# One core, fp32 decoder in split precision: two blocks' wide products behind each other, then both blocks' narrow ones, and later stages

## The chip, the cores and the metric

The kernel runs on one core of a Trainium2 chip. The metric is the device time of one execution in microseconds (us). One core has a matrix engine (TensorE, PE in the profile, with PEld for its weight loads), a vector engine (VectorE, DVE), a scalar engine (ScalarE, ACT), GpSimd (POOL) and SyncE (SP), which issues most transfers here. Each engine takes its own queue in order; they wait for each other by semaphores.

## The reference

Two decoder layers on 256 tokens of width 2048, all in fp32. Layer 0 has forgetting attention ("FoX": 32 heads of 64, a bias from a running sum of log-sigmoids), layer 1 attention in a window of 128 (32 query heads, 4 key/value heads, a learned sink per head, partial rotary). Both have a SiLU gate and an output projection.

```python
for i in range(DEPTH):
    h = rmsnorm(x, norm_g[i])
    if i % N_MIXERS == 0:
        p = h @ fox_w_in[j]            # q, k, v, gate, forget: 2048 x 8224
        ...
        y = fox_attention(q, k, v, log_f)
        w_out = fox_w_out[j]
    else:
        p = h @ swa_w_in[j]            # q, k, v, gate: 2048 x 4608
        ...
        y = swa_attention(q, k, v, swa_sinks[j])
        w_out = swa_w_out[j]
    y = y * jax.nn.silu(gate)
    x = x + y @ w_out
return rmsnorm(x, final_g)
```

## The kernel before

**Products.** Every fp32 operand is split into a high and a low half (two fp32r numbers), and a product keeps three of the four partial products. A `Unit` is 256 columns of an output; its 16 k-tiles come in parts of at most four. A part's weights are loaded by SP (`load`, L188 to L208), ACT casts the high half (L204), DVE subtracts to get the low half (L205). `block(unit, p, c)` (L210 to L248) does one part for one half `c` of the unit's 256 rows or columns: for each k-tile a **wide** matmul, 128x512, of the high stationary half with both halves of the moving operand side by side, and then for each k-tile a **narrow** one, 128x256, of the low stationary half with the high moving half. A block of four k-tiles is thus four wide and four narrow matmuls into one PSUM tile `acc`. After a unit's last part, `consume` is called: ACT copies the low columns out (L252), DVE adds, and what follows depends on the unit (q, k, v, gate, output). Units whose moving operand is the weight (v) read `acc<-w,xs` in the profile; the others read `acc<-xs,w`; in the output projections `ys` stands in place of `xs`. Matmuls are issued in one line (L75), transposes in L78.

**The order.** PE's order is the program's. The main loop (L876 to L889) takes the stream of (unit, part) and for each one emits half 0 of that part, and then half 1 of the part before it; only the last unit of the stream is done otherwise. So four wide, four narrow of one block are followed by four wide, four narrow of another. Inside a block `tick` (L104) is called after every second matmul: a block of four k-tiles is four **steps**. `after(n, f)` puts `f` n steps later; this is how the attention's stages are laid between the products. The other engines' order is set by the scheduler when the program is built; what a stage emits has a higher priority there (`HP`, L26).

**The stages of FoX.** When the first half of a group's k is consumed, `attend` (L404) puts off the two pairs of heads of the group (8 groups of 4 heads) by a table: `FOX_FIRST` for group 0, `FOX_NEXT` for group 1, `FOX_DUE` for the rest, `SWA_DUE` in layer 1. An entry (s, t) stands for: scores `s` after s steps, transposes `t` after t steps (the second head's four steps later); the third entry is when the values' products (`psy`) are done. `s` (L338) does two 128x512 matmuls into two PSUM tiles `ps_s`, DVE adds the bias (L347) and reduces (L333). The second block of keys (`s_first`, L353) follows `SECOND` = 8 steps later: two 128x256 matmuls into one `ps_s`, DVE add and reduce (L358, L333), then the softmax: L533 and L534 on DVE, four exponentials on ACT (L290), the reciprocal (L298) and four normalising products (L301) on DVE. The `ps_s` pool has two buffers. `t` (L363) transposes three blocks of the normalised `st` into `pt` (L78), ACT copies them (L369). The v unit's `consume` scales by ACT into `vg` (L462) and adds by DVE (L463), once for each half.

**Between the layers**, after each output row ACT and DVE split the new `x` for layer 1 (L155, L156), ACT squares it (L599), GpSimd sums the squares (L605); `norm` is put off by 10 steps after the last row (L629) and begins with the `ps_n` matmuls over that sum.

Of the kernel before, what the change touches and what calls it, by code (L numbers as in the profile page):

```python
# [36 lines left out]
SCALE_DUE = 8  # L37


FOX_DUE = ((16, 44), (48, 74), 106)  # L40
FOX_FIRST = ((60, 88), (86, 114), 128)
FOX_NEXT = ((28, 56), (58, 88), 112)
SWA_DUE = ((16, 40), (44, 64), 74)

SECOND = 8
WBUFS = 5
# [7 lines left out]
def trunk(  # L54
# [19 lines left out]
    def mm(*args, **kw):  # L74
        tc.keep_in_program_order(nc.tensor.matmul(*args, **kw))  # L75
# [24 lines left out]
    due = {}  # L100

    def after(steps, fn):
        due.setdefault(clock[0] + max(steps, 1), []).append(fn)

    def tick():
        clock[0] += 1
        for fn in due.pop(clock[0], ()):
            with tc.high_priority(HP):
                fn()
# [19 lines left out]
    def inv_rms(sums, name, columns, ps):  # L129
        for i, a in enumerate(sums):  # L130
            mm(ps[:, 0:S], ones, a, start=i == 0, stop=i == len(sums) - 1)
        n = S
        if columns:
            n = S + 2
            for th in range(2):
                for i, a in enumerate(sums):
                    mm(
                        ps[:, S + th : S + th + 1], a[:, th * P : (th + 1) * P], ones[:, 0:1],
                        start=i == 0, stop=i == len(sums) - 1,
                    )  # L140
        v = cpool.tile([P, S + 2], F32, tag="rms_v", name=f"v_{name}")[:, 0:n]
        nc.vector.tensor_scalar(v, ps[:, 0:n], 1.0 / D, EPS, op0=ALU.mult, op1=ALU.add)
        r = cpool.tile([P, S + 2], F32, tag="rms_r", name=f"r_{name}", bufs=2)[:, 0:n]
        nc.scalar.activation(r, v, AF.Ln)
        nc.scalar.activation(r, r, AF.Exp, scale=-0.5)

        t = cpool.tile([P, S + 2], F32, tag="rms_t", name=f"t_{name}")[:, 0:n]
        nc.vector.scalar_tensor_tensor(out=t, in0=r, scalar=-0.5, in1=r, op0=ALU.mult, op1=ALU.mult)
        nc.vector.tensor_mul(t, t, v)
        nc.vector.scalar_tensor_tensor(out=r, in0=t, scalar=1.5, in1=r, op0=ALU.add, op1=ALU.mult)  # L150
        return r

    def split_x(kt, layer):
        g = g_sb[:, layer, kt : kt + 1]
        nc.scalar.activation(xs[:, kt, 0, :], xT[:, kt, :], AF.Copy, scale=g)  # L155
        nc.vector.scalar_tensor_tensor(  # L156
            out=xs[:, kt, 1, :], in0=xT[:, kt, :], scalar=g, in1=xs[:, kt, 0, :].bitcast(F32),
            op0=ALU.mult, op1=ALU.subtract,
        )
# [50 lines left out]
    def block(unit, p, c):  # L210
        _, _, _, kt0, s = unit.parts[p]
        w, a = loaded[unit, p], unit.acts
        if p == 0:
            pool, tag = unit.acc
            unit.ps[c] = pool.tile([P, 512], F32, tag=tag, name="acc")
        n = unit.n if unit.kind == "tok" else S
        both, ps = unit.ps[c], unit.ps[c][:, 0:n]
        cs = slice(c * P, (c + 1) * P)
        def operands(i):

            kt = kt0 + i
            if unit.kind == "tok":
                return a[:, kt, 0, cs], a[:, kt, 1, cs], w[:, i]
            return w[:, i, 0, cs], w[:, i, 1, cs], a[:, kt]

        first, last = kt0 == 0, kt0 + s == KT
        ops = [operands(i) for i in range(s)]
        if unit.halves:

            for i, (sh, _, mv) in enumerate(ops):  # L230
                mm(both, sh, mv.rearrange("p h n -> p (h n)"), start=first and i == 0, stop=False)
                if i % 2:
                    tick()
            if s % 2:
                tick()
            for i, (_, sl, mv) in enumerate(ops):
                mm(ps, sl, mv[:, 0, :], start=False, stop=last and i == s - 1)
                if i % 2:
                    tick()
        else:  # L240
            for i, (sh, sl, mv) in enumerate(ops):
                mm(ps, sh, mv[:, 0, :], start=first and i == 0, stop=False)
                mm(ps, sl, mv[:, 0, :], start=False, stop=False)
            for i, (sh, _, mv) in enumerate(ops):
                mm(ps, sh, mv[:, 1, :], start=False, stop=last and i == s - 1)
                tick()
        if p == len(unit.parts) - 1:
            unit.consume(c, unit.ps[c])  # L248

    def low_half(ps):  # L250
        s = work.tile([P, S], F32, tag="row", name="half", bufs=4)
# [62 lines left out]
    class Pair:  # L314
# [23 lines left out]
        def s(self):  # L338

            self.st = work.tile([P, 2, 3 * P], F32, tag="st", name="st")  # L340
            self.mx = work.tile([P, 2, 2], F32, tag="mx", name="mx")
            rng, qb = BLK[1]
            pss = [ps_s.tile([P, 512], F32, tag="S", name="ps_s") for _ in range(2)]
            for hh in range(2):
                self.product(pss[hh], hh, qb, S)
            for hh in range(2):
                nc.vector.tensor_add(self.st[:, hh, rng], pss[hh][:, S:], self.bias[:, hh, rng])  # L347
                self.reduce(pss[hh][:, 0:S], hh, rng, qb)
            after(SECOND, self.s_first)

        def s_first(self):

# [15 lines left out]
                group.pts[hh] = work.tile([P, 2, 3 * P], F32, tag=f"pts{hh}", name="pts", bufs=1)  # L368
            nc.scalar.copy(group.pts[hh][:, self.j, :], pt[:, 0 : 3 * P])  # L369

        def later(self, group, s, t):
            after(s - BIAS, self.early)
            after(s, self.s)
            after(t, lambda: self.t(0, group))
            after(t + 4, lambda: self.t(1, group))
# [25 lines left out]
    class Group:  # L401


        def attend(self, kt, due, shared):  # L404
            self.pts = [None, None]
            for j, (s, t) in enumerate(due[0:2]):
                self.pair(j).later(self, s, t)
            after(due[2], lambda: self.values(kt, shared))

        def values(self, kt, shared):  # L410
# [56 lines left out]
    class FoxGroup(Group):  # L467
# [13 lines left out]
        def k(self, c, ps):  # L481
# [11 lines left out]
            if c == 0:  # L493
                due = {0: FOX_FIRST, 1: FOX_NEXT}.get(self.g, FOX_DUE)
                self.attend(2 * self.g, due, False)
# [101 lines left out]
    def square_into(sums, m):  # L597
        s = work.tile([P, S], F32, tag="row", name="sq", bufs=4)
        nc.scalar.activation(s, xT[:, m, :], AF.Square)  # L599
        if m == 0:  # L600
            acc = cpool.tile([P, S], F32, tag="ssq", name="acc", bufs=2)
            sums.append(acc)
            nc.gpsimd.tensor_copy(acc, s)  # L603
        else:
            nc.gpsimd.tensor_add(sums[0], sums[0], s)  # L605
# [5 lines left out]
    def to_layer1(m):  # L611
        split_x(m, 1)
        square_into(sums1, m)
        if m == KT - 1:

            def norm():
                nonlocal swa
                fox_scope.__exit__(None, None, None)
                swa = ctx.enter_context(tc.tile_pool(name="swa", bufs=2))
                state["r1"] = r = inv_rms(  # L620
                    sums1, "n1", True, ps_s.tile([P, 512], F32, tag="S", name="ps_n1")
                )
                rope = swa.tile([P, 2, S], F32, name="rope_c", bufs=1)
                nc.sync.dma_start(out=rope, in_=rope_d)
                nc.vector.tensor_mul(rope, rope, r[:, 0:S].unsqueeze(1).to_broadcast([P, 2, S]))
                state["rr"] = rope
                after(20, tail_residual)

            after(10, norm)  # L629

# [78 lines left out]

    fox_units = units
    first_out = out_units(fox_out_d, to_layer1)


# [32 lines left out]
    class SwaGroup(Group):  # L748
# [6 lines left out]
        def q(self, c, ps):  # L755
# [3 lines left out]
            if c == 0:  # L759
                self.attend(2 * self.u, SWA_DUE, True)  # L760

# [32 lines left out]
    last_out = out_units(swa_out_d, to_end)  # L794
# [46 lines left out]
    start = [(u, p) for p in range(2) for u in (v0, q0, k0)] + [(v0, 2), (v0, 3), (q0, 2), (k0, 2)]  # L841
# [7 lines left out]
    def fetch(upto):  # L849
        while fetched[0] < min(upto, len(stream)):  # L850
            load(*stream[fetched[0]])
            fetched[0] += 1
# [20 lines left out]
    sink = cpool.tile([P, H], F32, name="sink")  # L873
    state["sink"] = sink

    prev = None  # L876
    for i, (u, p) in enumerate(stream):
        fetch(i + 1 + LOOK)
        if u is last_out[7]:
            if p == 0:  # L880
                block(*prev, 1)
            block(u, p, 0)
            continue
        block(u, p, 0)
        if prev is not None:
            block(*prev, 1)
        prev = (u, p)
    for p in range(len(last_out[7].parts)):
        block(last_out[7], p, 1)  # L889


# ---- launch: one core; the host only lays arrays out
# [62 lines left out]
```

## Time and profile before

| | |
|---|---|
| median of 3 runs | 840.53 us (839.79 to 840.77) |
| profiled execution | 840.97 us, of which the traced span is 838.8 us |
| mean granted TensorE clock | 0.997 |
| PE busy, matmuls | 826.1 us, 98% of the span, 4906 |
| DVE busy | 670.3 us, 80% |
| ACT busy | 543.6 us, 65% |
| waits of PE, all | 6.9 us |

A timeline row reads: start (us from the span's start), us, engine, line, operation, output<-inputs, shape of the first instruction and the number of instructions put together in the row; in brackets the engine's idle time before it and who ended it. A matmul's listed end is modelled and lies past the start of the next one; spacing is read from starts. Steps are not marked in the profile; a block of four k-tiles is eight matmuls.

### The profile page before, as it was taken

The page shows a single profiled execution, that of the slowest core. Times are in us where ns is not written, and L with a number is a line of the kernel's source. Part 1 is how long each engine was busy: PE and PEld are TensorE (multiplying, and loading weights), DVE is VectorE, ACT ScalarE, POOL GpSimd, SP SyncE. Part 2 cuts the span into 40 slices and gives each one's busy share as a digit, 9 for nine tenths or more (in the row PEclk, how much of TensorE's full clock was granted, in tenths as well). Part 3 has the DMA queues.
Part 4 walks back from the last instruction along what each step waited for, and adds up shares of the span by engine and source line. Part 5 has one row for each costly group of instructions (what it writes and reads, how often), then busy time and mean ns, then how long its engine had stood idle before and what let it go on. Part 6 is the DMA issues. An engine that isn't in the chain of part 4 may idle for free.

```text
span 838.8 us, 13409 instructions
## 1 busy us (share of the span) xinstructions
PE 826.1 (98%) x4906; PEld 715.7 (85%) x4906; DVE 670.3 (80%) x1424; ACT 543.6 (65%) x1062; POOL 61.1 (7%) x93
## 2 busy tenths in 40 slices
PE   8999999999999999999999999999999999999996
PEld 7888888888888888888888888888888888888885
DVE  5899888779696887968658778788898889876755
ACT  6687776667575675757546565567766776665652
POOL 1011100100000010000002110000000000001311
PEclk9999999999999999999999999999999999999998
DMA  8666554655555465544475554544444445346522
GB/s 275 229 227 237 191 181 171 216 185 204 157 206 183 164 221 164 218 159 145 157 240 180 195 201 156 188 160 138 164 151 151 158 144 163 124 146 232 195 101 100
DMA packets 26672, 150.49 MB, mean 179 GB/s; under 512 B 3264, under 2 KB 5472, under 8 KB 11248
## 3 DMA queue, kind: packets, MB, share of 16 engines
q1 hardware_dynamic: 24192, 142.22, 49.5%
q0 software_dynamic: 1408, 6.36, 2.3%
q10 hardware_dynamic: 1008, 1.07, 0.4%
q8 instruction: 38, 0.62, 0.3%
q14 instruction: 26, 0.21, 0.1%
HBM read 147.50 MB, written 2.15 MB: 178 GB/s over the span
## 4 chain that ended last, share of the span: by engine, by line
PE 91%; DVE 3%; DMA 2%; ACT 2%; issue 1%; SPq 1%; DVEq 0%; ACTq 0%
PE acc L75 82%; PE ps_s L75 3%; PE psy L75 3%; PE pt L78 3%; DMA wraw<-in_fox_in_dram 1%; DVE w L205 1%; DMA wraw<-in_vf_dram 1%; ACT w L204 1%; SPq L199 1%; DVE xs L156 0%; ACT sq L818 0%; DVE scaled L699 0%; DVE ssq L819 0%; SPq L807 0%; DVE kk L490 0%
## 5 line engine op out<-in xcount | busy, mean ns | idle before, releaser
L75 PE MATMUL acc<-xs,w 128*128 128x256 f32 (+1 forms) x2624 | 485.2, 339 | 0.4 <-ACT w L204 0.3
L75 PEld LDWEIGHTS acc<-xs,w 128*128 128x128 f32 x2624 | 407.2, 189 | 61.3 <-issue 3.9
L205 DVE TENSOR_TENSOR w<-wraw,w 128x1024 fp32r<-128x1024 f32 (+4 forms) x275 | 324.1, 1183 | 96.3 <-ACT w L204 93.9
L204 ACT CAST w<-wraw 128x1024 fp32r<-128x1024 f32 (+4 forms) x275 | 277.8, 1015 | 153.2 <-PE acc L75 127.7
L75 PE MATMUL acc<-ys,w 128*128 128x512 f32 x960 | 170.4, 338 | 0.0
L75 PEld LDWEIGHTS acc<-ys,w 128*128 128x128 f32 x960 | 147.4, 189 | 21.5 <-issue 0.6
L75 PE MATMUL acc<-w,xs 128*128 128x256 f32 (+2 forms) x608 | 114.9, 334 | 1.9 <-ACT w L204 1.7
L75 PEld LDWEIGHTS acc<-w,xs 128*128 128x128 f32 x608 | 94.6, 189 | 14.8 <-ACT w L204 2.7
L252 ACT COPY half<-acc 128x256 f32<-128x256 f32 x112 | 41.2, 368 | 45.0 <-PE acc L75 44.3
L290 ACT ACTIVATE st<-st,mx 128x128 f32<-128x128 f32 (+1 forms) x128 | 56.6, 444 | 10.7 <-DVE mx L534 5.4
L369 ACT COPY pts<-pt 128x384 f32<-128x384 f32 x64 | 30.4, 475 | 14.5 <-PE pt L78 14.5
L75 PE MATMUL ps_s<-kk,q 128*128 128x512 f32 (+2 forms) x192 | 35.2, 306 | 1.3 <-DVE mx L333 1.3
L605 POOL TENSOR_TENSOR acc<-acc,sq 128x256 f32<-128x256 f32 x28 | 29.5, 1053 | 88.8 <-ACT sq L599 88.8
L301 DVE TENSOR_SCALAR st<-st,rl 128x128 f32<-128x128 f32 (+1 forms) x128 | 32.9, 321 | 1.1
L78 PE MATMUL pt<-ident,st 128*128 128x128 f32 x192 | 31.4, 272 | 0.0
L75 PEld LDWEIGHTS ps_s<-kk,q 128*128 128x128 f32 x192 | 26.2, 190 | 2.2 <-issue 1.7
L603 POOL COPY acc<-sq 128x256 f32<-128x256 f32 x2 | 1.9, 936 | 342.8 <-ACT sq L599 342.8
L521 POOL DMA_DIRECT2D bc<-negc_d x16 | 8.8, 553 | 221.0 <-DVE st L358 170.6
L78 PEld LDWEIGHTS pt<-ident,st 128*128 128x128 f32 x192 | 23.1, 140 | 1.9
L156 DVE SCALAR_TENSOR_TENSOR xs<-xT,g_sb,xs 128x256 fp32r<-128x256 f32 x32 | 22.0, 710 | 3.2 <-ACT xs L155 3.0
L310 ACT CAST q<-qT 64x256 fp32r<-64x256 f32 x32 | 12.8, 400 | 17.8 <-DVE qT L729 17.4
L290 ACT ACTIVATION_READ_ACCUMULATOR st<-st,mx 128x1 f32 x128 | 23.9, 187 | 0.0
(136 smaller groups left out, 590.7 us busy)
## 6 DMA issues: line engine op xcount, KB each, us to landing
wraw<-in_fox_in_dram SPq DMA_DIRECT2D x58, 1024.0 KB, 4.9
wraw<-in_swa_in_dram SPq DMA_DIRECT2D x36, 1024.0 KB, 4.9
wraw<-in_fox_out_dram SPq DMA_DIRECT2D x13, 1024.0 KB, 4.9
wraw<-in_swa_out_dram SPq DMA_DIRECT2D x13, 1024.0 KB, 4.9
bc<-negc_d POOLq DMA_DIRECT2D x16, 384.0 KB, 4.0
wraw<-in_fox_out_dram SPq DMA_DIRECT2D x6, 512.0 KB, 3.7
wraw<-in_swa_out_dram SPq DMA_DIRECT2D x6, 512.0 KB, 3.7
wraw<-in_fox_in_dram SPq DMA_DIRECT2D x4, 512.0 KB, 6.0
```

What stands on the lines that cost most here:

```text
L75: tc.keep_in_program_order(nc.tensor.matmul(*args, **kw))
L78: tc.keep_in_program_order(nc.tensor.transpose(out, in_, ident))
L156: nc.vector.scalar_tensor_tensor(out=xs[:, kt, 1, :], in0=xT[:, kt, :], scalar=g, in1=xs[:, kt, 0, :].bitcast(F32), op0=ALU.mult, op1=ALU. ...
L204: state["split"] = nc.scalar.copy(w[:, :, 0, :], raw)
L205: nc.vector.tensor_tensor(out=w[:, :, 1, :], in0=raw, in1=w[:, :, 0, :].bitcast(F32), op=ALU.subtract)
L252: nc.scalar.copy(s, ps[:, S : 2 * S])
L290: nc.scalar.activation(st[:, hh, rng], st[:, hh, rng], AF.Exp, bias=nm[:, qb, hh : hh + 1], accum_out=l[:, qb, hh : hh + 1],)
L301: nc.vector.tensor_scalar_mul(st[:, hh, rng], st[:, hh, rng], rl[:, qb, hh : hh + 1])
L310: nc.scalar.copy(q2[w, hh, :], t[w, :])
L369: nc.scalar.copy(group.pts[hh][:, self.j, :], pt[:, 0 : 3 * P])
L521: nc.gpsimd.dma_start(out=bc, in_=negc_d[h0 : h0 + 2, :].partition_broadcast(P))
L605: nc.gpsimd.tensor_add(sums[0], sums[0], s)
```

## The change

`block` no longer does its narrow matmuls at once: it returns them as a function. The main loop does the wide ones of half 0 of a part, then half 1 of the part before it (wide and narrow), then the narrow ones of half 0. The order of a slot "wide A, narrow A, wide P, narrow P" becomes "wide A, wide P, narrow P, narrow A". The steps are counted as before, so the `consume` of half 0 comes at the slot's end, four steps later, and that of half 1 two steps earlier. The tables move by four steps (a few entries otherwise), the first pair of group 0 has its second block of keys 16 steps behind the first instead of 8, and layer 1's norm is put off by 16 steps instead of 10. In the changed program the lines behind the edit are numbered higher by 7 or 8 (L290 becomes L297, L301 L308, L462 L470, L534 L542).

```diff
-FOX_DUE = ((16, 44), (48, 74), 106)
-FOX_FIRST = ((60, 88), (86, 114), 128)
-FOX_NEXT = ((28, 56), (58, 88), 112)
-SWA_DUE = ((16, 40), (44, 64), 74)
+FOX_DUE = ((20, 48), (52, 78), 110)
+FOX_FIRST = ((60, 92, 16), (88, 118), 132)
+FOX_NEXT = ((32, 60), (62, 92), 116)
+SWA_DUE = ((20, 44), (48, 68), 78)
...
+        def done():
+            if p == len(unit.parts) - 1:
+                unit.consume(c, unit.ps[c])
+
+        def narrow():
+            for i, (_, sl, mv) in enumerate(ops):
+                mm(ps, sl, mv[:, 0, :], start=False, stop=last and i == s - 1)
+                if i % 2:
+                    tick()
+            done()
...
-            for i, (_, sl, mv) in enumerate(ops):
-                mm(ps, sl, mv[:, 0, :], start=False, stop=last and i == s - 1)
-                if i % 2:
-                    tick()
...
+            return narrow
...
-            after(SECOND, self.s_first)
+            after(self.second, self.s_first)
...
-            after(10, norm)
+            after(16, norm)
...
-        block(u, p, 0)
+        narrow = block(u, p, 0)
         if prev is not None:
-            block(*prev, 1)
+            block(*prev, 1)()
+        narrow()
```

**First pair of group 0, PE.** `ps_s` are the scores (first 128x512, then the second block 128x256), `q_505` and `q_544` (`q_513` and `q_544` in the changed program) the q of the first and second pair, `pt` the transposes. Before:

```order
L75 MATMUL ps_s<-kk,q_505 128x512 x2
L75 MATMUL acc<-xs,w 128x256 x4
L75 MATMUL acc<-xs,w 128x512 x4
L75 MATMUL acc<-xs,w 128x256 x4
L75 MATMUL acc<-xs,w 128x512 x4
L75 MATMUL ps_s<-kk,q_505 128x256 x2
```

From there 20 narrow and 20 wide follow in fours, with the second pair's two 128x512 `ps_s` among them, up to the first `pt`. And now, up to the first `pt`:

```order
L75 MATMUL ps_s<-kk,q_513 128x512 x2
L75 MATMUL acc<-xs,w 128x256 x8
L75 MATMUL acc<-xs,w 128x512 x8
L75 MATMUL acc<-xs,w 128x256 x8
L75 MATMUL acc<-xs,w 128x512 x8
L75 MATMUL ps_s<-kk,q_513 128x256 x2
L75 MATMUL acc<-xs,w 128x256 x8
L75 MATMUL acc<-xs,w 128x512 x8
L75 MATMUL acc<-xs,w 128x256 x8
L75 MATMUL ps_s<-kk,q_544 128x512 x2
L75 MATMUL acc<-xs,w 128x512 x8
L78 MATMUL pt<-ident,st 128x128 x3
```

Between the first and the second block of the scores there are now 16 narrow and 16 wide instead of eight of each; between the second block and the transposes 16 narrow and 18 wide instead of 20 and 22.

**Second pair of group 3, PE**, where the v unit (`acc<-w,xs`) ends with its second half, up to the transposes of both heads. Before:

```order
L75 MATMUL acc<-xs,w 128x512 x4
L75 MATMUL acc<-xs,w 128x256 x4
L75 MATMUL acc<-w,xs 128x512 x4
L78 MATMUL pt<-ident,st 128x128 x3
L75 MATMUL acc<-w,xs 128x256 x4
L75 MATMUL acc<-xs,w 128x512 x4
L78 MATMUL pt<-ident,st 128x128 x3
```

Now:

```order
L75 MATMUL acc<-xs,w 128x512 x4
L75 MATMUL acc<-w,xs 128x512 x4
L75 MATMUL acc<-w,xs 128x256 x4
L75 MATMUL acc<-xs,w 128x256 x4
L75 MATMUL acc<-xs,w 128x512 x8
L75 MATMUL acc<-xs,w 128x256 x4
L78 MATMUL pt<-ident,st 128x128 x3
```

The transposes stood ahead of v's last narrow matmuls; now they stand behind them, with four narrow, eight wide and four narrow between.

**The same place on ACT:** the four exponentials (L290 before, L297 now) and the copies of v (L462, L470). Before:

```order
L204 CAST w<-wraw 128x4x256
L290 ACTIVATE st,l<-st,mx 128x128
L290 ACTIVATE st,l<-st,mx 128x256
L290 ACTIVATE st,l<-st,mx 128x128
L290 ACTIVATE st,l<-st,mx 128x256
L462 ACTIVATE vg<-acc,r_n_487 128x256
L204 CAST w<-wraw 128x4x256
L369 COPY pts<-pt 128x384
L462 ACTIVATE vg<-acc,r_n_487 128x256
```

Now:

```order
L204 CAST w<-wraw 128x4x256
L470 ACTIVATE vg<-acc,r_n_487 128x256 x2
L297 ACTIVATE st,l<-st,mx 128x128
L297 ACTIVATE st,l<-st,mx 128x256
L297 ACTIVATE st,l<-st,mx 128x128
L297 ACTIVATE st,l<-st,mx 128x256
L204 CAST w<-wraw 128x4x256 x2
L376 COPY pts<-pt 128x384 x2
```

Both copies of v, the second half's too, stand ahead of the exponentials now.

More of the change, by code (lines that the diff above doesn't have):

```diff
@@ L235, in block @@
                 tick()
-            for i, (_, sl, mv) in enumerate(ops):
-                mm(ps, sl, mv[:, 0, :], start=False, stop=last and i == s - 1)
-                if i % 2:
-                    tick()
[L240 to L248, printed above, removed]
+            return narrow
+        for i, (sh, sl, mv) in enumerate(ops):
+            mm(ps, sh, mv[:, 0, :], start=first and i == 0, stop=False)
+            mm(ps, sl, mv[:, 0, :], start=False, stop=False)
+        for i, (sh, _, mv) in enumerate(ops):
+            mm(ps, sh, mv[:, 1, :], start=False, stop=last and i == s - 1)
+            tick()
+        done()
+        return lambda: None
     def low_half(ps):
@@ L369, in t, with later @@
             nc.scalar.copy(group.pts[hh][:, self.j, :], pt[:, 0 : 3 * P])
-        def later(self, group, s, t):
+        def later(self, group, s, t, second):
+            self.second = second
             after(s - BIAS, self.early)
@@ L405, in attend @@
             self.pts = [None, None]
-            for j, (s, t) in enumerate(due[0:2]):
-                self.pair(j).later(self, s, t)
+            for j, (s, t, *second) in enumerate(due[0:2]):
+                self.pair(j).later(self, s, t, *(second or [SECOND]))
             after(due[2], lambda: self.values(kt, shared))
@@ L880, in trunk @@
             if p == 0:
-                block(*prev, 1)
-            block(u, p, 0)
+                block(*prev, 1)()
+            block(u, p, 0)()
             continue
-        block(u, p, 0)
+        narrow = block(u, p, 0)
         if prev is not None:
-            block(*prev, 1)
+            block(*prev, 1)()
+        narrow()
         prev = (u, p)
     for p in range(len(last_out[7].parts)):
-        block(last_out[7], p, 1)
+        block(last_out[7], p, 1)()
 def _units(w, n, per):
```

## The prediction

> **What bounds the kernel now.** I read the page's busy row first, then the chain that ended last, then the waits of PE.
>
> ```profile
> span 838.8 us, 13409 instructions
> PE 826.1 (98%) x4906; PEld 715.7 (85%) x4906; DVE 670.3 (80%) x1424; ACT 543.6 (65%) x1062; POOL 61.1 (7%) x93
> PE 91%; DVE 3%; DMA 2%; ACT 2%; issue 1%; SPq 1%; DVEq 0%; ACTq 0%
> ```
> ```profile
> PE rows L75 <- DVE tail L686: 2.5, 1, 2.5
> PE acc L75 <- ACT w L204: 2.0, 3, 0.9
> PE ps_s L75 <- DVE mx L333: 1.3, 1, 1.3
> PE warm L75 <- DVE ones L115: 1.1, 1, 1.1
> ```
>
> PE is busy for 98% of the span and is 91% of the chain, so the end is the number of matmuls times their spacing, plus what PE waits. The four wait rows (us in total, times, longest) add up to 6.9 us. No single cure is worth more than 2.5 us, while any new wait of PE is paid in full, because there is no idle time for it to fall into. The clock is granted nearly in full (0.997 in the table above). The change leaves the number of matmuls, transfers, casts and copies as it is; it can act in two ways only: by the spacing of matmuls in another order, and by waits that go or come.
>
> **Term 1: longer runs of wide and of narrow matmuls.** The two forms, and three pieces of PE's timeline (start, us, then the instructions):
>
> ```profile
> L75 PE MATMUL acc<-xs,w 128*128 128x512 f32 x1312 | 361.9, 396 | 0.3 <-ACT w L204 0.3
> L75 PE MATMUL acc<-xs,w 128*128 128x256 f32 x1312 | 213.0, 283 | 0.1
> ```
> ```profile
> 236.24 0.63 PE L75 MATMUL ps_s<-kk,q 128*128 128x512 f32 x2
> 236.70 2.95 PE L75 MATMUL acc<-xs,w 128*128 128x512 f32 x16
> 239.49 0.43 PE L75 MATMUL ps_s<-kk,q 128*128 128x256 f32 x2
> 239.75 4.37 PE L75 MATMUL acc<-xs,w 128*128 128x512 f32 x24
> 243.96 1.56 PE L75 MATMUL acc<-w,xs 128*128 128x512 f32 x8
> ```
> ```profile
> 817.91 5.92 PE L75 MATMUL acc<-w,ys 128*128 128x256 f32 x48
> 823.68 0.50 PE L75 MATMUL ps_cols<-ones,acc 128*128 128x1 f32 x4
> ```
> ```profile
> 202.33 0.64 PE L75 MATMUL acc<-w,xs 128*128 128x256 f32 x4
> 202.80 0.40 PE L75 MATMUL ps_s<-kk,q 128*128 128x256 f32 x2
> ```
>
> A row's form is that of its first instruction: the x24 are 12 wide and 12 narrow in fours. From 239.75 to 243.96 they take 4.21 us, 350.8 ns for a wide and a narrow together. Four narrow take 202.80 - 202.33 = 0.47 us, 117.5 ns each (118.5 below), which leaves 232 for a wide. 48 narrow in a row, with no wide among them, take 823.68 - 817.91 = 5.77 us, 120.2 each: a long narrow run is no faster than a run of four. For wide ones there is only the piece at 236.24: ten wide (two of them ps_s, so six in a row) and eight narrow in 239.49 - 236.24 = 3.25 us against 10 x 232 + 8 x 118.5 = 3.27, 0.02 less. In the order of the instructions PE goes from a wide run to a narrow one 488 times before and 207 times after; about 240 runs of four are joined in pairs. If each joining gave the 16 ns that lie between that piece and a like one at 248.73 (9 ns), the change would win 240 x 16 = 3.8 us; if narrow ones go from 118.5 to 120 each, it loses 240 x 11 ns = 2.6. I take **0**, nearest to the 48-in-a-row, and keep -3.8 and +2.6 as ends.
>
> The Trainium skill, page "TensorE: Matmul & The Clock Gate", section "Back-to-back issue gap", gives an isolated matmul's gap as its width over 2.4 plus 2.5 ns, 215.8 and 109.2 ns here, and says that in a stream weight load and matmul set the spacing together; neither form knows its neighbour's width. By that rule term 1 is 0 and the grouping buys nothing; the trace's 232 and 118.5 are larger than both figures, and only the independence from the order is used.
>
> **Term 2: the old wait at 68 us goes.** First pair of group 0, PE's timeline, then DVE's:
>
> ```profile
> 65.18 0.63 PE L75 MATMUL ps_s<-kk,q 128*128 128x512 f32 x2
> 65.65 2.94 PE L75 MATMUL acc<-xs,w 128*128 128x256 f32 x16
> 69.86 0.47 PE L75 MATMUL ps_s<-kk,q 128*128 128x256 f32 x2 [1.27 <-DVE mx L333]
> ```
> ```profile
> 70.18 6.26 PE L75 MATMUL acc<-xs,w 128*128 128x256 f32 x36
> ...
> 77.66 0.49 PE L78 MATMUL pt<-ident,st 128*128 128x128 f32 x3
> ```
> ```profile
> 69.98 0.09 DVE L333 DVE_READ_ACCUMULATOR2_ANT mx<- 128x1 f32 x1
> 69.98 0.69 DVE L269 TENSOR_TENSOR gt<-gt,gate_e 128x512 f32<-128x512 f32 x1
> 70.58 0.42 DVE L476 TENSOR_TENSOR q<-acc,half 128x256 f32<-128x256 f32 x1
> 70.91 0.42 DVE L358 TENSOR_TENSOR st<-ps_s,bc 128x256 f32<-128x256 f32 x1
> ```
>
> After the 16 matmuls (8 x 0.351 = 2.81 us from 65.65) PE could go on at 68.45 and does at 69.86: 1.4 us lost, since the third ps_s buffer comes free only when DVE has reduced the first. With 16 steps between, PE has 16 wide and 16 narrow (5.6 us) to do after the two ps_s, so the second block's matmuls stand at 65.18 + 0.93 (four more wide matmuls ahead of s) + 6.08 = 72.2, against reduces that end at 70.07 + 0.93 = 71.0, or 71.6 if the gate's product (0.69), which the new order puts ahead of them, delays them. **-1.4**; nothing comes back unless DVE falls behind by another 0.6 us.
>
> **Term 3: what is late next there.** In exchange the way from the second block to the transposes shrinks. Before, 20 narrow and 22 wide lie between (7.47 us, 70.18 to 77.66). After, 16 narrow and 18 wide (the order rows): 1.90 + 4.18 = 6.07. The chain that must fit is:
>
> ```profile
> 75.97 0.18 DVE L298 RECIPROCAL rl<-l 128x4 f32<-128x4 f32 x1
> 76.06 0.54 DVE L478 TENSOR_TENSOR q<-q,r 128x256 f32<-128x256 f32 x1
> 76.52 1.15 DVE L301 TENSOR_SCALAR st<-st,rl 128x128 f32<-128x128 f32 x4
> ```
>
> The first head is normalised after half of L301, at about 77.1 to 77.2, so before it had 0.5 us to spare of 7.47. It needs 7.0 and will have 6.07: a wait of **+0.9** at the first transposes. Ends: 0, if DVE's other work (L269, L476, L478 and a weight's L205 stand inside the chain) moves out of it; 2.3, if another L205 (1.2 us) and more of the second pair's adds get in ahead of the reciprocal.
>
> **Term 4: second pairs of groups 2 to 7.** Group 3 before, on ACT, DVE and PE:
>
> ```profile
> 205.69 0.40 ACT L290 ACTIVATE st<-st,mx 128x128 f32<-128x128 f32 x1
> ...
> 207.38 0.18 ACT L290 ACTIVATION_READ_ACCUMULATOR st<-st,mx 128x1 f32 x1
> 207.47 0.45 ACT L462 ACTIVATE vg<-acc,r_n 128x256 f32<-128x256 f32 x1
> ```
> ```profile
> 207.59 0.18 DVE L298 RECIPROCAL rl<-l 128x4 f32<-128x4 f32 x1 [0.64 <-ACT st L290]
> 207.81 1.01 DVE L301 TENSOR_SCALAR st<-st,rl 128x128 f32<-128x128 f32 x4
> ```
> ```profile
> 209.58 0.49 PE L78 MATMUL pt<-ident,st 128*128 128x128 f32 x3
> ```
>
> Before, the exponentials (L290) run ahead of both copies of v (L462), and the first head is ready at 207.81 + 0.5 = 208.3, 1.2 us ahead of its transposes. The change brings v's second half six steps behind its first instead of twelve, and the softmax four steps later: in ACT's order both vg copies now stand ahead of the exponentials. ACT takes its queue in order, so the exponentials wait for v's last narrow matmul. From there PE has, by the order rows, 4 narrow, 8 wide, 4 narrow to the transposes: 8 x 0.351 = 2.81 us. ACT and DVE need: the matmul's end (283 - 118 = 0.17 behind its successor's start), vg 0.35 to 0.45, exponentials 207.56 - 205.69 = 1.87, then reciprocal and first head 0.75, and hand-overs of 0.03 each: 3.2 to 3.3. PE waits 0.4 to 0.5 each time; with L534 on DVE, which the new order puts behind the first L463 (0.48), up to 0.8. Behind the waiting transposes stands all of PE. I take 0.6 x 6 = **+3.6**; ends 0.2 and 0.8 each, 1.2 to 4.8. The second head, four steps later (1.4 us against 0.5 of L301), waits for nothing.
>
> **Term 5: first pairs of groups 2 to 7.** Their scores' second block stands 6.8 us ahead of the transposes instead of
>
> ```profile
> 190.22 0.40 PE L75 MATMUL ps_s<-kk,q 128*128 128x256 f32 x2
> ...
> 197.47 0.49 PE L78 MATMUL pt<-ident,st 128*128 128x128 f32 x3
> ```
>
> 7.25, and some of DVE's work on k leaves the chain in return. **+0.3** in all; ends 0 and 6 x 0.25 = 1.5.
>
> **Term 6: layer 1's norm.** It is called six steps later because x's last rows are.
>
> ```profile
> 501.93 0.82 POOL L605 TENSOR_TENSOR acc<-acc,sq 128x256 f32<-128x256 f32 x1 [2.31 <-ACT sq L599]
> ```
> ```profile
> 503.06 0.59 PE L75 MATMUL ps_n<-acc,ones 128*128 128x256 f32 x2
> ```
>
> GpSimd's sum ends at 502.75, 0.3 before PE needs it. After, both halves' copies, casts and squares follow each other closely on ACT, a cast (1.05 us) between them: **+0.5**, ends 0 and 0.9.
>
> **At nothing:** layer 2's attention (its stages move four steps with their consumers, and a pair's slack there covers them; end +1), the start (bound by transfers and casts whose order stays; 0.4 either way), and the tail, whose blocks keep their order. SP's loads are issued by slot as before, and a weight buffer comes free four narrow matmuls (0.47 us) sooner.
>
> **Sum:** 0 - 1.4 + 0.9 + 3.6 + 0.3 + 0.5 = **+3.9** on the profiled execution's 840.97, which lies 0.44 above the median of 840.53: **844.4**.
>
> **The rivals.** *A, the new waits are hidden:* if the scheduler's order does not bind because the exponentials' inputs and v's come together anyway, terms 3 to 6 shrink to 1.4 and cancel term 2: 840.5. For it: 1.2 us of slack in term 4; against it: the order rows. *B, the other side, faster:* wide runs of eight keep what the piece at 236.24 shows, 16 ns at each of 240 joinings, -3.8, and the old wait goes, -1.4, against new waits of at most 2.5: 837.8. It decides as soon as a joining is worth 10 ns and terms 3 to 6 stay under 2; against it stand the 48 narrow at 120.2. *C, waits spread:* term 4 at its upper end, first pairs at 1.5, term 3 at 2.3, the norm at 0.9, layer 2 at 1 and narrow ones at 120: 840.5 - 1.4 + 4.8 + 1.5 + 2.3 + 0.9 + 1 + 1.3 = 851.
>
> **How the numbers follow.** About 0.2%, 1.7 us, is what a measurement of this kernel tells from no change: 838.9 to 842.2. Forecast 0.60 (842.2 to 849), A 0.20, B 0.12, C 0.08. The range leaves out B and C: 839.0 to 848.8. Faster is B, 0.12; same is A and the forecast's lowest tail, 0.23; slower 0.65.
>
> **What would show it.** Right: no PE wait on DVE's L333 any more; six waits of pt on DVE's normalisation of 0.2 to 0.8 us at second pairs, one near 78.5 us, one of ps_n on GpSimd; 24 alternating products still 4.2 us. Wrong: if pt never waits, or if eight wide in a row take clearly under 1.85 us, term 4 or term 1 is the one that failed.

## The result, and the profile after

The changed kernel takes 846.38 us (median of 4 runs, 846.09 to 847.28) against 840.54 before (four runs now): 5.84 us more, ratio 1.0069 with a 95% interval of 1.0056 to 1.0081. It is slower, as forecast, by 5.8 us where 3.9 were forecast, and inside the range. How far the terms of the sum were right is another matter, and most of what follows is about that.

The profiled execution took 847.28 us, the slowest of the four, with a span of 845.2. The page after, its span, busy row and chain, and all waits of PE (us in total, times, longest):

```profile
span 845.2 us, 13412 instructions
PE 828.8 (98%) x4906; PEld 719.2 (85%) x4906; DVE 666.8 (79%) x1424; ACT 537.8 (64%) x1062; POOL 60.8 (7%) x93
PE 72%; DVE 17%; ACT 7%; issue 2%; DMA 1%; SPq 1%; POOL 0%; DVEq 0%; ACTq 0%; POOLq 0%
```
```profile
PE pt L78 <- DVE st L308: 5.2, 10, 1.7
PE rows L75 <- DVE tail L694: 2.5, 1, 2.5
PE warm L75 <- DVE ones L115: 1.1, 1, 1.1
PE acc L75 <- ACT w L204: 0.9, 3, 0.5
PE acc L75 <- DVE w L205: 0.4, 1, 0.4
PE ps_n L75 <- POOL acc L613: 0.2, 1, 0.2
```

The busy shares hardly differ from before. The chain does: PE falls from 91% to 72%, and DVE and ACT take 17% and 7%, since ten times the transposes wait for the softmax and the chain passes over to it. Apart from waits for the first weights, the row of pt is new with 5.2 us and that of ps_n with 0.2; the old wait for L333 (1.3) is gone.

Not all is in the list of waits, so I counted from the starts: for each matmul the time to the next one's start beyond 231 ns (wide), 119 (narrow) and 80 (a transpose), summed by stretch, us:

| stretch (us) | what runs there | before | changed | tuned (below) |
|---|---|---|---|---|
| 0 to 50 | start | 7.8 | 6.5 | 6.7 |
| 50 to 75 | group 0, scores | 1.8 | 0.2 | 0.2 |
| 75 to 100 | group 0, transposes | 0.5 | 4.1 | 1.0 |
| 100 to 150 | group 1 | 0.7 | 0.7 | 1.1 |
| 150 to 425 | groups 2 to 7 | 3.0 | 6.2 | 2.2 |
| 425 to 500 | output projection | 0.2 | -0.1 | -0.2 |
| 500 to 550 | norm, layer 2 begins | 1.2 | 1.2 | 1.0 |
| 550 to 750 | layer 2's attention | 6.2 | 9.2 | 5.7 |
| 750 to end | last projection, tail | 3.6 | 3.6 | 3.4 |
| sum | | 25.0 | 31.4 | 21.2 |

The sums (of the unrounded values) differ as the spans do (838.8, 845.2, 834.9). The stretches are cut by the clock, so a few tenths of the same work can fall on the other side of a border, and every row holds its share of the gain in spacing (next paragraph). Three stretches carry the loss: group 0's transposes, groups 2 to 7, and layer 2.

**Spacing.** PE's timeline in the output projection, where no stage lies between the products, before and then after (a row and the one behind it):

```profile
420.18 76.50 PE L75 MATMUL acc<-ys,w 128*128 128x256 f32 x436
496.52 1.57 PE L75 MATMUL acc<-xs,w 128*128 128x512 f32 x8
```
```profile
426.97 73.35 PE L75 MATMUL acc<-ys,w 128*128 128x256 f32 x420
500.15 1.09 PE L75 MATMUL acc<-xs,w 128*128 128x512 f32 x4
```

Before, 436 matmuls take 496.52 - 420.18 = 76.34 us, 350.2 ns for a wide and a narrow; after, 420 take 73.18, 348.5. So the longer runs are worth 1.7 ns a pair here; over 2048 wide matmuls in fours (1312 + 480 + 256) that would be 3.5 us. The whole kernel gains less. Summed over all products whose spacing lies within 45 ns of the usual 231 and 119 (4090 and 4072 of 4192), the products themselves take **2.5 us** less. By starts, a run of eight wide has a median of 1841 ns against twice 929 for fours, and eight narrow 953 against twice 473: the wide win 17 ns, the narrow lose 7. With 239 runs of eight wide and 224 of eight narrow in the changed program this too is 4.1 - 1.6 = 2.5.

**Group 0.** PE, then DVE:

```profile
64.75 0.62 PE L75 MATMUL ps_s<-kk,q 128*128 128x512 f32 x2
65.20 5.75 PE L75 MATMUL acc<-xs,w 128*128 128x256 f32 x32
70.79 0.40 PE L75 MATMUL ps_s<-kk,q 128*128 128x256 f32 x2
...
78.94 0.70 PE L78 MATMUL pt<-ident,st 128*128 128x128 f32 x3 [1.71 <-DVE st L308]
```
```profile
71.87 1.22 DVE L205 TENSOR_TENSOR w<-wraw,w 128x1024 fp32r<-128x1024 f32 x1
73.01 0.42 DVE L365 TENSOR_TENSOR st<-ps_s,bc 128x256 f32<-128x256 f32 x1
...
74.96 1.22 DVE L205 TENSOR_TENSOR w<-wraw,w 128x1024 fp32r<-128x1024 f32 x1
76.10 0.15 DVE L542 TENSOR_TENSOR mx<-cq,mx 128x4 f32<-128x4 f32 x1
...
78.19 0.18 DVE L305 RECIPROCAL rl<-l 128x4 f32<-128x4 f32 x1 [0.92 <-ACT st L297]
...
78.60 1.01 DVE L308 TENSOR_SCALAR st<-st,rl 128x128 f32<-128x128 f32 x4
```

The second block no longer waits (70.79 is 16 wide and 16 narrow behind the scores). But DVE starts on it only at 73.01, two us after the matmuls, behind a weight's L205, and a second L205 stands ahead of L542 and so ahead of the exponentials. PE waits 1.71 us for the first head.

**Second pair of group 3**, ACT, DVE, PE:

```profile
211.20 0.47 ACT L470 ACTIVATE vg<-acc,r_n 128x256 f32<-128x256 f32 x1 [1.37 <-PE acc L75]
211.58 0.39 ACT L297 ACTIVATE st<-st,mx 128x128 f32<-128x128 f32 x1
...
213.24 0.20 ACT L297 ACTIVATION_READ_ACCUMULATOR st<-st,mx 128x1 f32 x1
```
```profile
213.47 0.18 DVE L305 RECIPROCAL rl<-l 128x4 f32<-128x4 f32 x1 [1.27 <-ACT st L297]
213.68 1.01 DVE L308 TENSOR_SCALAR st<-st,rl 128x128 f32<-128x128 f32 x4
```
```profile
211.00 2.95 PE L75 MATMUL acc<-xs,w 128*128 128x256 f32 x16
214.12 0.61 PE L78 MATMUL pt<-ident,st 128*128 128x128 f32 x3 [0.16 <-DVE st L308]
```

This is term 4 step by step: ACT sits idle 1.37 us for v's last narrow matmuls, copies v at 211.20, and only then come the exponentials, the reciprocal and the products. Sixteen matmuls take 2.8 us from 211.00, so PE was ready at 213.80 and went on at 214.12. The three transposes behind the wait then take 0.61 us instead of the 0.49 that they take without one: by starts they lie 0.17 us apart instead of 0.11.

**Layer 2**, a second pair in its attention: before, then after, each PE and DVE (L394 and L402 are the first reduces of the scores):

```profile
602.48 7.16 PE L75 MATMUL acc<-xs,w 128*128 128x512 f32 x40
609.48 0.49 PE L78 MATMUL pt<-ident,st 128*128 128x128 f32 x3
```
```profile
602.78 1.23 DVE L205 TENSOR_TENSOR w<-wraw,w 128x1024 fp32r<-128x1024 f32 x1
603.92 0.28 DVE L394 CUSTOM_DVE_ANT_0 st<-ps_s,smask 128x128 f32<-128x128 f32 x1
```
```profile
609.00 7.59 PE L75 MATMUL acc<-xs,w 128*128 128x512 f32 x40
617.18 0.61 PE L78 MATMUL pt<-ident,st 128*128 128x128 f32 x3 [0.59 <-DVE st L308]
```
```profile
609.95 0.69 DVE L272 SCALAR_TENSOR_TENSOR gate_e<-gt,gate_e 128x512 f32<-128x512 f32 x1 [1.12 <-ACT gate_e L271]
610.89 1.23 DVE L205 TENSOR_TENSOR w<-wraw,w 128x1024 fp32r<-128x1024 f32 x1 [0.24 <-ACT w L204]
612.03 0.28 DVE L402 CUSTOM_DVE_ANT_0 st<-ps_s,smask 128x128 f32<-128x128 f32 x1
```

Between scores and transposes lie 40 matmuls before and after. Before, DVE reduces 1.4 us after the scores, behind a weight's L205; after, 3.0 us, since the gate's product (L272), which itself waits 1.1 us for ACT, now stands ahead of that L205. Three of layer 2's second pairs wait so, 0.7, 1.1 and 1.1 us by the starts.

### The profile page after: what moved, and what is told of

It is laid out like the page before. It is cut to its first block, busy times and chain, and to the rows that moved or that the text cites. A ratio compares the mean times of both kernels' runs of the same rounds, so it can differ in the third digit from the quotient of the medians.

```text
span 845.2 us, 13412 instructions
## 1 busy us (share of the span) xinstructions
PE 828.8 (98%) x4906; PEld 719.2 (85%) x4906; DVE 666.8 (79%) x1424; ACT 537.8 (64%) x1062; POOL 60.8 (7%) x93
## 4 chain that ended last, share of the span: by engine, by line
PE 72%; DVE 17%; ACT 7%; issue 2%; DMA 1%; SPq 1%; POOL 0%; DVEq 0%; ACTq 0%; POOLq 0%
PE acc L75 65%; DVE w L205 5%; ACT st L297 4%; PE psy L75 2%; PE pt L78 2%; PE ps_s L75 2%; DVE st L402 2%; DVE st L308 2%; DVE q L318 1%; DMA wraw<-in_vf_dram 1%; ACT w L204 1%; DMA wraw<-in_fox_in_dram 1%; DVE gt L284 1%; DVE gt L283 1%; DVE rot L733 1%
## 5 line engine op out<-in xcount | busy, mean ns | idle before, releaser
L75 PE MATMUL acc<-xs,w 128*128 128x512 f32 (+1 forms) x2624 | 484.7, 339 | 0.4 <-ACT w L204 0.4
L205 DVE TENSOR_TENSOR w<-wraw,w 128x1024 fp32r<-128x1024 f32 (+4 forms) x275 | 323.9, 1182 | 98.0 <-ACT w L204 95.5
L75 PE MATMUL acc<-ys,w 128*128 128x256 f32 (+1 forms) x960 | 170.3, 338 | 0.0
L75 PE MATMUL acc<-w,xs 128*128 128x512 f32 (+2 forms) x608 | 114.5, 334 | 1.1 <-ACT w L204 0.5
L297 ACT ACTIVATE st<-st,mx 128x128 f32<-128x128 f32 (+1 forms) x128 | 56.6, 444 | 27.8 <-DVE mx L777 16.9
L78 PE MATMUL pt<-ident,st 128*128 128x128 f32 x192 | 33.1, 279 | 5.2 <-DVE st L308 5.2
L308 DVE TENSOR_SCALAR st<-st,rl 128x128 f32<-128x128 f32 (+1 forms) x128 | 33.6, 326 | 0.9
L431 ACT CAST ys<-gt 128x512 fp32r<-128x512 f32 x16 | 9.9, 620 | 27.9 <-DVE gt L430 27.9
L297 ACT ACTIVATION_READ_ACCUMULATOR st<-st,mx 128x1 f32 x128 | 24.1, 188 | 0.0
```

The lines of the kernel that those rows point to most:

```text
L78: tc.keep_in_program_order(nc.tensor.transpose(out, in_, ident))
L205: nc.vector.tensor_tensor(out=w[:, :, 1, :], in0=raw, in1=w[:, :, 0, :].bitcast(F32), op=ALU.subtract)
L297: nc.scalar.activation(st[:, hh, rng], st[:, hh, rng], AF.Exp, bias=nm[:, qb, hh : hh + 1], accum_out=l[:, qb, hh : hh + 1],)
L308: nc.vector.tensor_scalar_mul(st[:, hh, rng], st[:, hh, rng], rl[:, qb, hh : hh + 1])
L431: nc.scalar.copy(out[:, :, 0, :], y)
```

## The experiments

Medians in us; each ratio is against the kernel before timed beside it (840.74 for the tables alone, the order alone, 94 steps and all stages later, 840.51 for the others). A difference to the changed kernel is against its 846.38, which was not timed again beside them; the kernel before varied by 0.2 us between these timings.

**The tables alone** (the old order of the blocks):

```diff
-        narrow = block(u, p, 0)
+        block(u, p, 0)()
         if prev is not None:
             block(*prev, 1)()
-        narrow()
```

> The new tables (stages four steps later, 16 steps in group 0, norm at 16) with the old order of the blocks. Theory: the new tables are harmless but for group 0's transposes (they wait 1 to 2 us there, the old wait of 1.4 at 68 us is gone) and there is no gain in spacing, so 350.2 ns for a wide and a narrow in the output projection as before: 840 to 843 us. Rival (the tables alone bring all the new waits): 845 or more, with second pairs and layer 2 waiting as in the changed kernel.

841.74, ratio 1.0017 (1.0007 to 1.0026). The old wait is gone, pt of group 0 waits 1.5 us, and the list has no other new wait at a stage: as the theory had it. The late stages alone cost 1.0 us. By starts group 0 has little part in that (1.5 less in 50 to 75 us, 1.8 more in 75 to 100); 1.0 more stands from 150 to 425 us, in delays too short for the list.

**The order alone** (all old tables, norm at 10):

```diff
-FOX_DUE = ((20, 48), (52, 78), 110)
-FOX_FIRST = ((60, 92, 16), (88, 118), 132)
-FOX_NEXT = ((32, 60), (62, 92), 116)
-SWA_DUE = ((20, 44), (48, 68), 78)
+FOX_DUE = ((16, 44), (48, 74), 106)
+FOX_FIRST = ((60, 88), (86, 114), 128)
+FOX_NEXT = ((28, 56), (58, 88), 112)
+SWA_DUE = ((16, 40), (44, 64), 74)
...
-            after(16, norm)
+            after(10, norm)
```

> The new order of the blocks with all old tables. Theory: spacing of 348.5 ns for a wide and a narrow as in the changed kernel, about 2050 x 1.7 ns = 3.5 us less than before; the waits at group 0's transposes and at second pairs and in layer 2 come from the later stages, so most of them are not there: 836 to 840 us. Rival (the order makes the waits, because the two halves' consumers come six steps apart): spacing gained, waits of 3 us or more at pt all the same, 841 to 846.

854.45, ratio 1.0175 (1.0154 to 1.0195): my theory fell, and the rival too was far too low. PE's timeline at group 3's first scores:

```profile
190.22 0.47 PE L75 MATMUL ps_s<-kk,q 128*128 128x512 f32 x1 [0.26 <-DVE kk L499]
191.11 0.47 PE L75 MATMUL ps_s<-kk,q 128*128 128x512 f32 x1 [0.42 <-DVE kk L499]
```

The scores now wait for k, whose two halves reach DVE six steps apart instead of twelve: DVE begins on the one at 186.2 and on the other at 187.1 us (L491), ahead of the first half's L499. Layer 2's norm waits too (2.5 us for GpSimd's sum), and so does pt (3.1 us). The spacing is gained here too (2.1 us by the sum over all products), and the waits eat it up. The losses come from the order, and the later tables take most of them away. I had the roles reversed.

**Group 0's first transposes two steps later:**

```diff
-FOX_FIRST = ((60, 92, 16), (88, 118), 132)
+FOX_FIRST = ((60, 94, 16), (88, 118), 132)
```

> The changed kernel with the first pair's transposes of group 0 at 94 instead of 92 steps. Theory: the 1.9 us wait there shrinks by two steps (0.7 us) to about 1.2, and the stretch at half clock behind it (80.4 to 83.4 us, worth about 1.6 us) goes too, since a wait of 1.3 us in the kernel before brought none: 846.4 - 2.3 = 844.1. Rival (the half clock has another cause than the length of the wait): 846.4 - 0.7 = 845.7, half clock still there.

845.26, 1.1 less, between the two. The longest wait of pt is 1.1. The half clock is gone, but that says little: see the last section.

**All waiting stages later** (pt of group 0 at 98, second pairs at 82, layer 2's transposes at 48 and 72 with values at 82, norm at 20):

```diff
-FOX_DUE = ((20, 48), (52, 78), 110)
-FOX_FIRST = ((60, 92, 16), (88, 118), 132)
+FOX_DUE = ((20, 48), (52, 82), 110)
+FOX_FIRST = ((60, 98, 16), (88, 118), 132)
...
-SWA_DUE = ((20, 44), (48, 68), 78)
+SWA_DUE = ((20, 48), (48, 72), 82)
...
-            after(16, norm)
+            after(20, norm)
```

> The changed kernel with the stages that wait put off: group 0's first transposes at 98, second pairs of groups 2 to 7 at 82 (values at 114... left at 110), layer 2's transposes four steps later (values at 82), norm at 20. Theory (the loss is nothing but waits of PE on stages that stand too close): first pair 3.5, second pairs 1.9, layer 2 3.0 and norm 0.5 go, 846.4 - 8.9 = 837.5, faster than both kernels. Rival (the chains only move along, or the copies and products behind them become late): 842 to 846.

843.40, ratio 1.0033 (1.0020 to 1.0046): 3.0 less than the changed kernel, a third of what was expected. Two waits had moved along: group 0's second pair (0.7 us at 105 us), and layer 2's values. PE and ACT there:

```profile
616.65 2.36 PE L75 MATMUL psy<-pts,vs 128*64 128x512 f32 x8
```
```profile
616.67 0.41 ACT L317 CAST q<-qT 64x256 fp32r<-64x256 f32 x1 [2.35 <-DVE qT L737]
616.98 0.47 ACT L376 COPY pts<-pt 128x384 f32<-128x384 f32 x1
```

The last copy of pt stands on ACT behind a cast of the next q, which waits for DVE; the eight `psy` matmuls take 2.36 us where the kernel before had 1.52. Before, the two heads' `psy` matmuls start in pairs, 14 ns apart; here the first head's begin at 616.65 and the second's only at 617.50, just after that copy ends at 617.45. By starts five of the layer's eight groups take 2.3 us instead of 1.45, which makes 4.5 and is more than the three waits before pt had cost.

**Second pairs of groups 2 to 7 alone, four steps later:**

```diff
-FOX_DUE = ((20, 48), (52, 78), 110)
+FOX_DUE = ((20, 48), (52, 82), 110)
```

> The changed kernel with the second pairs' transposes of groups 2 to 7 at 82 instead of 78 steps. Theory (ACT's exponentials stand behind v's second half): the six waits of 0.32 us before pt go, 846.4 - 1.9 = 844.5; the two vg copies stay ahead of the exponentials. Rival (the wait moves to the copies of pt or to the values' products): within 0.5 us of 846.4.

843.38, 3.0 less than the changed kernel. In the stretch from 150 to 425 us the excess falls from 6.2 to 3.5.

**Layer 2 alone:**

```diff
-SWA_DUE = ((20, 44), (48, 68), 78)
+SWA_DUE = ((20, 44), (48, 72), 86)
```

> The changed kernel with layer 2's second pairs at 72 instead of 68 steps and the values at 86 instead of 78, so that the last copy of pt has 10 steps instead of 6 before the values need it. Theory: the three waits of 0.7 to 1.1 us at layer 2's second transposes go and nothing takes their place, 846.4 - 3.0 = 843.4. Rival (as with all stages later, the copy of the last pt stands on ACT behind a q cast and the values' products wait for it): 845.5 or more.

842.85, 3.5 less. The three waits are gone and none takes their place (excess of 5.8 instead of 9.2 from 550 to 750 us).

**Group 0 alone:**

```diff
-FOX_FIRST = ((60, 92, 16), (88, 118), 132)
+FOX_FIRST = ((60, 98, 16), (88, 122), 136)
```

> The changed kernel with only group 0's transposes put off, to 98 and 122 (values at 136). Theory: its wait of 1.7 us and what little is left at 120 go, 846.4 - 2.0 = 844.4; six steps are 2.1 us, so nothing is left before pt of the first pair. Rival (as with all stages later, the second pair waits instead): 845.3 or more.

845.86, 0.5 less: the rival. The wait of 1.7 is gone, and further on stands

```profile
97.37 0.48 PE L75 MATMUL ps_s<-kk,q 128*128 128x256 f32 x2 [0.91 <-DVE mx L340]
```

the same kind of wait for a `ps_s` buffer that the change had cured in the first pair, now in the second.

**Group 0's second block 8 behind again:**

```diff
-FOX_FIRST = ((60, 92, 16), (88, 118), 132)
+FOX_FIRST = ((60, 92), (88, 118), 132)
```

> The changed kernel with group 0's second block of keys 8 steps behind the first again. Theory (one wait in exchange for the other): the 1.7 us wait before the transposes goes and the old one before the second block's ps_s comes back with 1.3 to 1.5 us, as the third ps_s buffer is not free sooner: 846.0 to 846.6, the same within the measurement. Rival (the wait before the transposes was the price of 16, and the later start alone cures the old wait): 844.6, no wait on L340.

845.31, 1.1 less than the changed kernel; neither case held. PE's timeline:

```profile
69.72 0.48 PE L75 MATMUL ps_s<-kk,q 128*128 128x256 f32 x2 [0.80 <-DVE mx L340]
```

The old wait comes back, but with 0.8 instead of 1.27, and pt of group 0 waits for nothing. In this order and with pt at 92 the 16 steps cost more than they cure.

**The old order, with its old wait cured** (the order and the other tables as before the change; against the kernel before):

```diff
-FOX_FIRST = ((60, 88), (86, 114), 128)
+FOX_FIRST = ((60, 98, 16), (88, 120), 132)
```

> The kernel before, with its order and its tables, but group 0's first pair with the second block of keys 16 steps behind and its transposes at 98 (second pair's at 120). Theory: the old wait of 1.4 us at 68 us goes and nothing comes: 840.6 - 1.4 = 839.2. Rival (the chain only moves along): 840.6 or more. Against the run with the new order and all stages later, the difference is then the spacing: 3.5 us.

839.80, ratio 0.9992 (0.9983 to 1.0001): half of the 1.4 at best, and not clear of no change.

**The new order, tuned:**

```diff
-FOX_DUE = ((20, 48), (52, 78), 110)
-FOX_FIRST = ((60, 92, 16), (88, 118), 132)
+FOX_DUE = ((20, 52, 12), (52, 82), 110)
+FOX_FIRST = ((60, 98, 16), (88, 122), 136)
...
-SWA_DUE = ((20, 44), (48, 68), 78)
+SWA_DUE = ((20, 44), (48, 72), 86)
...
-            after(16, norm)
+            after(20, norm)
```

> The new order of the blocks with every stage that waited put off, as far as the traces showed waits: group 0 transposes at 98 and 122, other first pairs with the second block 12 behind and transposes at 52, second pairs at 82, layer 2 at 72 with values at 86, norm at 20. Theory: what is left of the change is its gain in spacing (3.5 us) and the old wait of 1.4: 840.6 - 4.9 = 835.7, faster than both. Rival (the six steps between the two halves' consumers cost DVE and ACT more than a table can give back): 839 to 843.

837.58, ratio 0.9967 (0.9954 to 0.9979): faster than both kernels, by 2.9 us than the one before, though 1.9 short of the 835.7 that was expected. Of that, 1.0 is the spacing, put at 3.5 and worth 2.5. It is 2.2 below the old order with the old wait cured, near to what the spacing is worth.

**And group 0's second pair later still** (against the run above):

```diff
-FOX_FIRST = ((60, 98, 16), (88, 122), 136)
+FOX_FIRST = ((60, 98, 16), (88, 126), 138)
```

> The tuned version with group 0's second pair four steps later still, at 126 (values at 138). Theory: its last waits before pt (0.4 and 0.3 us at 104 us) go: 837.6 - 0.6 = 837.0. Rival (nothing more to win there, the products behind become late): 837.6 to 838.2.

837.42, ratio 0.9957 (0.9944 to 0.9969): against the run above not told apart; the last wait of pt (0.24 there) is gone, and one of 0.5 for a `ps_s` buffer stays (0.57 there).

## Why the prediction was right, term by term

The direction and the mechanism were right: PE has no idle time, so each new wait is paid. The nearness of 3.9 to 5.8 is partly luck: two terms at 0 were wrong by 2.5 and 3.3 us, in opposite directions.

- **Term 1, spacing: 0 forecast, -2.5 measured.** The step that failed is the choice of "nearest to the 48-in-a-row". That row has narrow matmuls alone, and it told the narrow part rightly (they lose); the wide part stood in the piece at 236.24, from which the prediction itself had worked out -3.8. It kept -3.8 and +2.6 as two ends of one term, but wide and narrow runs both grow, so both parts come: -4.1 and +1.6 were measured. By the prediction's own sign (eight wide clearly under 1.85 us) 1.841 is a near thing. The Trainium skill's formula in "TensorE: Matmul & The Clock Gate", section "Back-to-back issue gap", knows no neighbour's width. Here the order counts for half a per cent: 350.2 against 348.5 ns for the same two matmuls.
- **Term 2, the old wait: -1.4 forecast.** It went, as the timeline shows (1.6 less in 50 to 75 us). What it is worth is less: curing it in the old order won 0.7 us at best.
- **Term 3, the new wait there: +0.9 forecast, 1.7 measured**, inside the ends and by the mechanism named for the upper one (another L205 and the second pair's adds ahead of the reciprocal). Its price in the time is smaller than the wait: removing it won 0.5 us, since the second pair then waits.
- **Term 4, second pairs: +3.6 forecast, 3.0 when undone.** Mechanism, place and number of waits were right; a single one was put at 0.6 us. By starts each wait is 0.32 us, and the transposes behind it take 0.12 longer, 0.44 together and 2.6 for six. Lined up product by product, the changed kernel falls behind the run with 82 steps by 2.8 us in six such jumps.
- **Term 5, first pairs: +0.3 forecast, 1.3 to 1.5 measured, elsewhere.** Not pt but the second block's `ps_s` waits, a quarter of a microsecond in each of six groups; DVE's reduce of the first head there (L340) ends just before, at 144.80 in group 2. PE, group 2:

```profile
141.92 2.95 PE L75 MATMUL acc<-xs,w 128*128 128x256 f32 x16
144.95 0.47 PE L75 MATMUL ps_s<-kk,q 128*128 128x256 f32 x2
```

Eight narrow and eight wide take 0.95 + 1.84 = 2.79 us, so 144.95 is 0.24 late. The prediction looked for this wait in group 0 alone, where it was listed. In the tuned version, with 12 steps, the gap is gone.
- **Term 6, norm: +0.5 forecast, 0.5 measured.** Listed with 0.2; by starts the two matmuls of `ps_n` come and go 0.5 later than before. The run with norm at 10 shows 2.5 there, so the 16 was needed.
- **Layer 2, at nothing: 0 forecast (end +1), +3.3 measured** (three waits of 3.0 together, and the slower transposes behind them), 3.5 when undone. This is the worst step: "its stages move four steps with their consumers, and a pair's slack there covers them". The slack was that of the order before; what stands ahead of the reduces on DVE in the new order (the gate's product and an L205) was not looked up for this stage, as it was for FoX.

Taken apart by kind, the two profiled spans differ by: -2.5 for the spacing; outside of it -1.2 in the start, -1.5 and +3.6 in group 0 (some 1.6 of this is the half clock of this one execution: 4.1 in that stretch against 2.4 and 2.6 in two runs with the same wait), +4.0 from 150 to 425 us, +3.3 in layer 2 and +0.8 in all the rest, the norm's 0.5 among it. That makes 6.5, against 845.2 - 838.8 = 6.4. The start was put at nothing; its row varies from run to run by as much as it differs here (6.5 to 7.8 in these traces). The sum is of one pair of traces, and a check of sizes, not of every term.

Of the rivals, B's mechanism was real (the wide runs gave 4.1 where it had 3.8, but the narrow ones took 1.6 back), and its condition, new waits under 2, did not hold; the tuned version, without most of these waits, stands where B put the change (837.6 against 837.8). A, hidden waits, did not occur. Of C, group 0's wait came with 1.7 and layer 2's with 3.3 where it had 1.

## What to carry to other kernels

Where the engine that bounds is 98% busy, an order that wins 0.3% in spacing is paid for with every stage that was placed by the old order: look up for each stage, in the new order of each engine, what now stands ahead of its first instruction on DVE and ACT, and not only for the stages with known waits. An operation moved later by some steps takes its wait to the next one in its chain, so undo them together and look at the trace again. When a bound of a term is worked out from the very instructions that the change multiplies (wide runs here), it is nearer than a long row of another kind; and two ends that belong to two kinds of instruction, both of which change, are to be added, not chosen between.

## What the runs showed of the hardware

**A stretch at half clock after a wait of 1.7 us, in one execution only.** The changed kernel's profile by stretches of two us (busy time and count of PE, PEld, DVE, ACT, POOL, then the granted clock, DMA share, GB/s), and then the run with layer 2 later, whose wait at the same place was 1.82 us:

```profile
79.00:81.00 2.00, 2.00 (x13) 1.88 (x14) 1.74 (x4) 1.36 (x3) 0.00 (x0) 0.78 0.72 266
81.00:83.00 2.00, 2.00 (x8) 1.72 (x7) 1.69 (x3) 1.66 (x5) 0.00 (x0) 0.50 0.09 37
83.00:85.00 2.00, 2.00 (x11) 1.71 (x10) 1.79 (x9) 0.20 (x1) 0.56 (x1) 0.87 0.65 176
```
```profile
80.06 0.70 PE L78 MATMUL pt<-ident,st 128*128 128x128 f32 x3 [1.82 <-DVE st L308]
```
```profile
81.00:83.00 2.00, 2.00 (x15) 1.86 (x15) 1.45 (x2) 1.95 (x4) 0.00 (x0) 1.00 0.31 127
83.00:85.00 2.00, 2.00 (x14) 1.79 (x13) 1.92 (x8) 1.20 (x4) 0.49 (x1) 1.00 0.30 61
```

At clock 0.50 a wide matmul was followed by the next after 427 ns instead of 231, and 8 matmuls ran in 2 us instead of 15. By the three rows' clocks the stretch lasted about 0.9 + 2.0 + 0.5 = 3.4 us. The waits of 1.5 to 1.82 us at this place in three other runs brought none, so the length of the wait alone does not decide it, and my expectation for the run at 94 steps rested on too little. The Trainium skill, page "TensorE: Matmul & The Clock Gate", "Part 1: The HAM clock gate", has half rate after an idle window of about 3.4 us, whose phase is free; the spacing at half rate agrees (it gives 426.7 ns), a wait of 1.7 us as the cause does not, and what set it off stays open. The half clock is the likely reason that this execution is the slowest of the four, 0.7 to 1.2 above the others.

**Runs of wide matmuls get faster as they go on, runs of narrow ones slower.** In runs of eight in the changed kernel the medians from one start to the next are 233, 236, 228, 232, 231, 227, 227, 227 ns for wide ones and 114, 119 and then 120 ns for narrow ones; in runs of four before, 234, 234, 231, 230 and 117, 119, 119, 120. What limits the first wide ones was not tested.
